# Two mixers' outputs token-major and normalised tile by tile, and an output projection that runs by tile, in a two-layer diffusion backbone

## The chip, the cores and the metric

The kernel runs on one core of one Trainium2 chip. The core has five engines that run at the same time, each with an instruction stream of its own that it works through in order: TensorE (PE in the profile; PEld is its loading of stationary operands), VectorE (DVE), ScalarE (ACT), GpSimd (POOL) and SyncE (SP, which here only issues DMAs). Matmul results go to PSUM, which has eight banks of 128 x 512 fp32. The metric is the time of one execution on the device, in microseconds (us).

## The reference

The kernel computes two trunk layers over 384 tokens: 128 of a prompt (tile 0) and 256 of a sample (tiles 1 and 2). The change lies in layer 0. There a mixer runs two groups of four heads beside each other, HGRN2 and gated DeltaNet, both in two directions; each head's output is RMS-normalised, multiplied by a gate, and all eight go through one output projection. Then follow a gated residual, a norm and an MLP.

```python
    oa_f, sa_f = hgrn_dir(f_fw, s_h[:, 0], False)
    oa_b, sa_b = hgrn_dir(f_bw, s_h[:, 1], True)
    o_a = _rmsnorm(oa_f + oa_b, gn_a) * jax.nn.silu(_heads(g_a, H_A).astype(f32))
    ...
    ob_f, sb_f = gdn_dir(a_fw, b_fw, 0, s_g[:, 0], False)
    ob_b, sb_b = gdn_dir(a_bw, b_bw, 1, s_g[:, 1], True)
    o_b = _rmsnorm(ob_f + ob_b, gn_b) * jax.nn.silu(_heads(g_b, H_B).astype(f32))
    o = jnp.concatenate([_merge(o_a), _merge(o_b)], axis=-1).astype(h.dtype)
    return (o @ w_out, ...
```

```python
        xp = xp + p_g1 * mp
        xs = xs + s_g1 * ms
        hp = _rmsnorm(xp, norm_g[l, 1]) * (1.0 + p_sc2) + p_sh2
        hs = _rmsnorm(xs, norm_g[l, 1]) * (1.0 + s_sc2) + s_sh2
        xp = xp + p_g2 * _mlp(hp, w_mlp1[l], w_mlp2[l])
        xs = xs + s_g2 * _mlp(hs, w_mlp1[l], w_mlp2[l])
```

## The kernel before

Precise products are made of three matmuls: each fp32 operand is split into a rounded part (hi) and a remainder (lo), and hi x hi, lo x hi and hi x lo are added up in PSUM. Weights are split on the fly (`split`, ACT in L211, DVE in L212) from a ring of three `raw` buffers into rings of four `whi` and four `wlo`. Plain fp32 matmuls appear in the profile as two instructions each.

A planner puts the instructions of each engine in their order: it takes what its own model holds to be ready, and among that what comes first in the program. The program's order in the mixer is the string `STEPS`: `h` advances the HGRN chain by one step, `d` the DeltaNet chain, `g0` to `g3` are the four blocks of output gates (`gate`, matmuls in `fm_block`, L647 to L649, then `evac_gate`, L1230 and L1231), `m` writes HGRN's part of the mixer's result. `ORDER` holds some matmul groups back: `("gate1", 0): [("out", 2)]` queues the first half of gate block 1 behind DeltaNet's output matmuls of tile 2. Blocks 0 and 1 are HGRN's gates, 2 and 3 DeltaNet's. All eight gate heads lie in `sg`, which is the memory of the residual stream `x` and, before that, of HGRN's keys; `x` is loaded again (`load_x`) once the gates have been used.

DeltaNet's chain is one long dependence: `gdn_attn` (L1015, L1017), `gdn_out(2)`, `gdn_out(1)`, two state steps of tile 0 (`gdn_step`, L1146 to L1177), `gdn_out(0)`. An output needs two rows of decay factors (`gdn_qg`, L1026 to L1031), then 16 or 32 small matmuls (L1188, L1191) into one bank of the tag `gd` (two banks, in turn), and one copy to SBUF (L1192). `hgrn_out` (L847 to L851) does the like with the two banks of `hg`. Both write the output with the head's features on the partitions and tokens along the row (feature-major).

So the RMS norm over features is a sum over partitions. `mix_out` makes it on TensorE, for all three tiles at once and one head at a time: squares (L1249), a matmul with a column of ones (L1251; for DeltaNet a second one with the squares of q, L1255, which carries the L2 norm's epsilon), a square root on ACT (L1258), a reciprocal on DVE (L1259), a matmul with a row of ones that spreads the factors over the partitions (L1263), a multiplication (L1265) and the split (L1266, L1267). POOL multiplies by the gates (L1256). HGRN's `mix_out` is step `m`; DeltaNet's comes after all gates.

`proj_residual` then projects with accumulators in banks 2, 3, 4 and 5 for tiles 0 and 1: for each quarter of the eight feature blocks, for both tiles, for both halves of the columns (L674 to L676). All four sums end at nearly the same time. Tile 2 follows, in pieces that `ORDER` queues behind the transposes of the next norm. `norm` calls `step(t)` for each tile, which finishes the residual (L1273, L1275), and then squares (L544), scales (L549, L550), transposes (L555), modulates (L560, L562) and splits (L564, L566, L567). The MLP's first two blocks of hidden units take tiles 0 and 1 first and tile 2 later (L1340 to L1342); their weights' splits are queued behind the norm of the first tile (`("w1", 0)`).

Of the kernel before, what the change touches and what calls it, by code (L numbers as in the profile page):

```python
# [17 lines left out]
P = 128  # L18
# [39 lines left out]
c0 h3 c1 h5 d2 h d2 h d h5 g0 g1 h d h m g2 g3 a3  # L58
# [49 lines left out]
class Trunk:  # L108
# [27 lines left out]
    def load_x(self):  # L136
        nc, i = self.nc, self.i
        nc.sync.dma_start(self.x[:, 0], i["x_prompt"][0])
        for t in range(2):
            nc.sync.dma_start(self.x[:, 1 + t], i["x_sample"][0, t * P:(t + 1) * P])  # L140
# [389 lines left out]
    def norm(self, A, B, tag, ready=None):  # L530
# [4 lines left out]
        for t in range(NT):  # L535
# [15 lines left out]
            for j in range(2):  # L551
                pt = self.ps([P, 4, P], "tmp")
                hf = self.sb([P, 4, P], self.tag_hf)
                for k in range(4):
                    self.mark["T", t, j] = nc.tensor.transpose(pt[:, k], xh[j][:, k * P:(k + 1) * P], self.c["ident"])  # L555
# [7 lines left out]
                if j:  # L563
                    self.mark["A", t] = nc.scalar.activation(hi.tiles[j][:, :, c], hf, AF.Copy)  # L564
                else:
                    nc.vector.tensor_copy(hi.tiles[j][:, :, c], hf)  # L566
                self.mark["D", t] = nc.vector.tensor_sub(lo.tiles[j][:, :, c], hf, hi.tiles[j][:, :, c].bitcast(F32))  # L567
# [273 lines left out]
    def hgrn_out(self, t, r, Sf, Sb):  # L841
# [17 lines left out]
    def mixer_tiles(self):  # L859
# [149 lines left out]
    def gdn_attn(self):  # L1009

        nc = self.nc
        for t in range(NT):
# [3 lines left out]
            for d in range(2):  # L1016
                nc.vector.tensor_mul(self.AT_[:, t, d], pk, self.AT_[:, t, d])  # L1017

# [122 lines left out]
    def gdn_step(self, t, d, S, want):  # L1141
# [28 lines left out]
        for h in range(4):  # L1170
            self.mark["s", t, d] = nc.tensor.matmul(pu[:, h], kt[:, h], ws[:, h], start=True, stop=True)
# [9 lines left out]
    def gdn_out(self, t, w, S):  # L1181
# [10 lines left out]
        nc.scalar.activation(self.vt[:, t], po, AF.Copy)  # L1192

    def gdn_steps(self):
# [15 lines left out]
        self.gdn_attn()  # L1210
        yield
# [12 lines left out]
    def evac_gate(self, n):  # L1224
# [3 lines left out]
        def f(pg):  # L1228
            s = self.cvt([P, T])
            nc.scalar.activation(s, pg, AF.Sigmoid)  # L1230
            nc.vector.scalar_tensor_tensor(self.sg[:, n], pg, self.prm[:, 12 + n // 4:13 + n // 4], s, op0=ALU.mult, op1=ALU.mult)  # L1231
        return f

    def mix_out(self, kind, y, tag):
# [3 lines left out]
        o = (self.oA, self.oB)[kind]  # L1238
        tt = lambda ap: ap.rearrange("p (t c) -> p t c", t=NT)

        one = self.mixc([P, 32], f"one{kind}")
        nc.gpsimd.memset(one, 0.0)
        nc.gpsimd.memset(one[:, 0:1], 1.0)
        e = self.mixc([P, 1], f"epsn{kind}")
        nc.gpsimd.memset(e, EPS * EPS * P if kind else EPS * P)
        st = self.ps([P, T], tag)
        for h in range(4):
            sq = self.g2([P, T])
            nc.scalar.activation(tt(sq), o[:, h], AF.Square, scale=P ** -0.5)  # L1249
            row = st[32 * h:32 * h + 32]  # L1250
# [554 lines left out]
```

## Time and profile before

| what | us |
|---|---|
| three runs | 1164.83, 1165.47, 1169.36 |
| their median | 1165.47 |
| the profiled execution, its own time | 1165.99 |
| its span, first to last instruction | 1164.2 |

The profiled execution lies 0.52 us above the median, and 1.79 us of it lie outside the span. The mean granted TensorE clock is 0.978 of full speed. The stretch of the change, from the last HGRN and DeltaNet outputs to the MLP's first matmuls, reaches from about 262 us to 404 us of the span. In the windows view each row gives a stretch, its length, and for each engine the busy time with the number of instructions in brackets (PE, PEld, DVE, ACT, POOL), then the granted clock, the busy share of the DMA engines and GB/s. In the timeline each row is a start, a length, an engine, a line of the kernel, the instruction, its output and inputs, and in brackets how long the engine had been idle and what ended that.

### The profile page before, as it was taken

The numbers are of one execution on the slowest core, as the hardware profiler recorded it, in microseconds if no ns is written. First come the engines' busy times: TensorE is split into PE (matmuls) and PEld (weight loads), VectorE is DVE, ScalarE is ACT, GpSimd is POOL, SyncE is SP. The second block draws the span as 40 slices with busy tenths as digits, with TensorE's granted clock in tenths as the row PEclk, the third lists the DMA queues.
The fourth block names the chain that finished last, engine by engine and source line by source line (L and its number), as shares of the span: only waits on it lengthen the run. The fifth ranks groups of instructions, "written<-read, shape, count | busy, mean of one in ns | idle before, by whom it ended". The sixth has DMA issues, their size and how long they took to land.

```text
span 1164.2 us, 17957 instructions
## 1 busy us (share of the span) xinstructions
PE 1102.8 (95%) x6853; PEld 940.6 (81%) x6853; DVE 766.5 (66%) x1179; ACT 493.6 (42%) x845; POOL 286.7 (25%) x309
## 2 busy tenths in 40 slices
PE   6989978998899799999999999999988999999998
PEld 3868767987866698988988878888767889999987
DVE  4587699895253788885899574877757773333333
ACT  4465323442452564334334353665635543333331
POOL 0054993231210302111112133433003011111102
PEclk9989988998998899999999999999999999999999
DMA  8954625341133287776777317665623964434301
GB/s 292 281 173 110 212 94 160 103 129 35 48 127 115 73 321 246 269 234 202 234 237 222 98 34 196 177 192 143 171 74 97 340 196 139 123 118 127 109 37 55
DMA packets 142090, 184.65 MB, mean 159 GB/s; under 512 B 36803, under 2 KB 113685, under 8 KB 142005
## 3 DMA queue, kind: packets, MB, share of 16 engines
q1 hardware_dynamic: 141685, 183.44, 50.5%
q8 instruction: 54, 0.88, 0.3%
q14 instruction: 31, 0.25, 0.1%
q10 hardware_dynamic: 320, 0.07, 0.0%
HBM read 171.53 MB, written 4.61 MB: 151 GB/s over the span
## 4 chain that ended last, share of the span: by engine, by line
PE 73%; DMA 7%; DVE 7%; POOL 7%; SPq 2%; issue 2%; ACT 1%; DVEq 0%; POOLq 0%; ACTq 0%
PE tmp L1341 7%; PE tmp L1342 7%; PE tmp L1340 7%; PE acc L1326 7%; PE acc L1327 7%; PE acc L1328 7%; POOL sm L1062 2%; POOL sm L1063 2%; DMA ada<-in_ada_w 2%; PE acc L647 2%; PE acc L648 2%; PE acc L649 2%; PE acc L675 2%; PE acc L674 2%; PE po L1715 2%
## 5 line engine op out<-in xcount | busy, mean ns | idle before, releaser
L212 DVE TENSOR_TENSOR wlo<-raw,whi 128x1024 fp32r<-128x1024 f32 x192 | 240.7, 1264 | 167.1 <-ACT whi L211 161.0
L211 ACT ACTIVATE whi<-raw 128x1024 fp32r<-128x1024 f32 x198 | 206.2, 1050 | 334.1 <-PE acc L1328 202.8
L1360 POOL TENSOR_TENSOR h<-h 128x384 f32<-128x384 f32 x56 | 66.9, 1195 | 426.4 <-ACT h L1357 423.7
L1327 PE MATMUL acc<-wlo,h 128*128 128x512 f32 x380 | 148.6, 391 | 0.0
L1326 PE MATMUL acc<-whi,h 128*128 128x512 f32 x380 | 146.1, 393 | 0.0
L349 DVE SCALAR_TENSOR_TENSOR adc<-adr,scz,adc 128x1024 f32<-128x1024 f32 x98 | 126.8, 1323 | 11.7 <-DMA adr<-in_ada_w 11.6
L1328 PE MATMUL acc<-whi,h 128*128 128x512 f32 x380 | 121.2, 391 | 0.0
L1326 PEld LDWEIGHTS acc<-whi,h 128*128 128x128 f32 x380 | 71.2, 188 | 19.7 <-ACT whi L211 5.0
L1340 PE MATMUL tmp<-hyA,whi 128*128 128x384 f32 (+1 forms) x256 | 83.8, 333 | 3.2 <-DVE hyA L566 3.2
L1341 PE MATMUL tmp<-hyA,whi 128*128 128x384 f32 (+1 forms) x256 | 84.8, 332 | 0.4 <-DVE hyA L567 0.4
L1340 PE MATMUL tmp<-hyB,whi 128*128 128x384 f32 (+1 forms) x256 | 83.7, 329 | 1.2 <-DVE hyB L566 1.2
L1341 PE MATMUL tmp<-hyB,whi 128*128 128x384 f32 (+1 forms) x256 | 84.0, 329 | 0.7 <-DVE hyB L567 0.7
L1342 PE MATMUL tmp<-hyA,wlo 128*128 128x384 f32 (+1 forms) x256 | 84.6, 332 | 0.0
L1327 PEld LDWEIGHTS acc<-wlo,h 128*128 128x128 f32 x380 | 71.4, 188 | 14.5 <-DVE wlo L212 0.8
L1342 PE MATMUL tmp<-hyB,wlo 128*128 128x384 f32 (+1 forms) x256 | 82.1, 328 | 0.0
L1328 PEld LDWEIGHTS acc<-whi,h 128*128 128x128 f32 x380 | 71.0, 188 | 13.7
L647 PE MATMUL acc<-hyA,whi 128*128 128x384 f32 x208 | 73.8, 355 | 1.4 <-DVE hyB L708 1.4
L648 PE MATMUL acc<-hyA,whi 128*128 128x384 f32 x208 | 71.9, 345 | 0.0
L649 PE MATMUL acc<-hyA,wlo 128*128 128x384 f32 x208 | 71.3, 344 | 0.0
L1361 DVE TENSOR_TENSOR h<-h,h 128x384 fp32r<-128x384 f32 (+2 forms) x72 | 38.4, 535 | 41.1 <-POOL h L1360 40.4
L1340 PEld LDWEIGHTS tmp<-hyA,whi 128*128 128x128 f32 x256 | 48.4, 191 | 4.5 <-ACT km L562 3.6
L1341 PEld LDWEIGHTS tmp<-hyA,whi 128*128 128x128 f32 x256 | 49.0, 191 | 1.6 <-DVE hyA L567 0.6
(464 smaller groups left out, 2402.5 us busy)
## 6 DMA issues: line engine op xcount, KB each, us to landing
raw<-in_w_mlp SPq DMA_DIRECT2D x128, 512.0 KB, 3.9
adr<-in_ada_w SPq DMA_DIRECT2D x80, 512.0 KB, 4.6
raw<-in_w_in_ab SPq DMA_DIRECT2D x34, 512.0 KB, 5.1
ada<-in_ada_w SPq DMA_DIRECT2D x32, 256.0 KB, 5.3
raw<-in_w_qkv_na SPq DMA_DIRECT2D x32, 256.0 KB, 3.5
raw<-in_w_out_ab SPq DMA_DIRECT2D x8, 512.0 KB, 5.3
m<-gs SPq DMA_DIRECT2D x8, 512.0 KB
raw<-in_w_qkv_na SPq DMA_DIRECT2D x8, 512.0 KB
```

Source lines behind the costliest of these rows:

```text
L211: self.nc.scalar.activation(hi, x, AF.Copy)
L212: (eng or self.nc.vector).tensor_tensor(lo, x, hi.bitcast(F32), op=ALU.subtract)
L349: nc.vector.scalar_tensor_tensor(acc[v], raw, s[v], acc[v], op0=ALU.mult, op1=ALU.add)
L647: nc.tensor.matmul(pg[n], whi(k)[:, c], hhi[:, k], start=(k == 0), stop=False)
L648: nc.tensor.matmul(pg[n], whi(k)[:, c], hlo[:, k], start=False, stop=False)
L649: nc.tensor.matmul(pg[n], wlo(k)[:, c], hhi[:, k], start=False, stop=(k == KT - 1))
L1326: nc.tensor.matmul(pg, shi, w2hi(n)[:, o], start=start, stop=False)
L1327: nc.tensor.matmul(pg, shi, w2lo(n)[:, o], start=False, stop=False)
L1328: nc.tensor.matmul(pg, slo, w2hi(n)[:, o], start=False, stop=last)
L1340: nc.tensor.matmul(pg[n], w1hi(k)[:, c], hhi[:, k, tc_], start=(k == 0), stop=False)
L1341: nc.tensor.matmul(pg[n], w1hi(k)[:, c], hlo[:, k, tc_], start=False, stop=False)
L1342: nc.tensor.matmul(pg[n], w1lo(k)[:, c], hhi[:, k, tc_], start=False, stop=(k == KT - 1))
```

## The change

The outputs of both mixers are computed token-major: the operands of the output matmuls change places, so that tokens lie on the partitions. The norm over features is then a sum along the row. `out_norm` makes it for each tile at the end of `hgrn_out` and `gdn_out`, reading the output from PSUM: four ACT squares with a sum each, a small DVE addition, a small power on POOL (`rsqrt`), and one DVE multiplication from PSUM to SBUF. The epsilon that comes from q is summed once for all tiles in `gdn_eps`, right behind `gdn_attn`. `mix_out` now runs for one tile: four transposes, a multiplication by the gates, the split. Where the gates lie in `sg` is swapped between the two groups. The projection's program order is one half of the features for tiles 2 and 1, then DeltaNet's `mix_out` for all three tiles, then the other half tile by tile; tile 0 comes last, and the first MLP takes the tiles in the same order 2, 1, 0. The accumulators get a sixth bank. Gate blocks 0 and 1 are held behind nothing any more, blocks 2 and 3 behind DeltaNet's outputs of tiles 2 and 1. The HGRN chain's last two steps move ahead of the gates. The marks that `norm` sets count tiles in the order in which they come. In layer 1 nothing changes but the order in which `proj_residual` takes its banks.

```diff
-    ("gate1", 0): [("out", 2)],
-    ("gate1", 1): [("s", 0, 0)],
-    ("gate2", 0): [("out", 0)],
-    ("proj", 0, 2, 1): [("T", 0, 0), ("T", 0, 1)],
-    ("proj", 1, 2, 0): [("T", 1, 0), ("T", 1, 1)],
+    ("gate2", 0): [("out", 2)],
+    ("gate3", 0): [("out", 1)],
+    ("proj", 0, 1): [("T", 0, 0), ("T", 0, 1)],
+    ("proj", 1, 0): [("T", 1, 0), ("T", 1, 1)],
...
-c0 h3 c1 h5 d2 h d2 h d h5 g0 g1 h d h m g2 g3 a3
+c0 h3 c1 h5 d2 h d2 h d h7 g0 g1 d m g2 g3 a3
...
-                self.mark["out", t] = nc.tensor.matmul(po[:, h], w[d][:, h], self.AT_[:, t, d, h], start=(d == 0), stop=last)
+                self.mark["out", t] = nc.tensor.matmul(po[:, h], self.AT_[:, t, d, h], w[d][:, h], start=(d == 0), stop=last)
             if S is not None:
                 for d in range(2):
-                    nc.tensor.matmul(po[:, h], S[d][:, h], qg[d][:, h], start=False, stop=(d == 1))
-        nc.scalar.activation(self.vt[:, t], po, AF.Copy)
+                    nc.tensor.matmul(po[:, h], qg[d][:, h], S[d][:, h], start=False, stop=(d == 1))
+        self.out_norm(1, t, po, self.vt[:, t])
...
+    def gdn_eps(self):
+        pq = self.ps([P, NT, 4], "gd")
+        for h in range(4):
+            q2 = self.g2([P, NT, P])
+            nc.scalar.activation(q2, self.kq[:, :, h, 1], AF.Square, scale=(EPS * P) ** 0.5)
+            for t in range(NT):
+                nc.tensor.matmul(pq[:, t, h:h + 1], q2[:, t], self.c["ones"][:, 0:1], start=True, stop=True)
+        self.qe = self.mixc([P, NT, 4], "qe")
+        nc.vector.tensor_scalar(self.qe, pq, EPS * EPS * P, None, op0=ALU.add)
...
+    def out_norm(self, kind, t, po, out):
+        ss, rs = self.sb([P, 4], "ss4"), self.sb([P, 4], "ss4")
         for h in range(4):
+            nc.scalar.activation(out[:, h], po[:, h], AF.Square, scale=P ** -0.5, accum_out=ss[:, h:h + 1])
+        if kind:
+            nc.vector.tensor_add(ss, ss, self.qe[:, t])
+        else:
+            nc.vector.tensor_scalar(ss, ss, EPS * P, None, op0=ALU.add)
+        self.rsqrt(rs, ss)
+        nc.vector.tensor_mul(out, po, rs.unsqueeze(2).broadcast_to([P, 4, P]))
+
+    def mix_out(self, kind, t, y, tag):
+        o = (self.qa, self.vt)[kind][:, t]
+        c = slice(t * P, (t + 1) * P)
+        pt = self.ps([P, 4, P], tag)
         for h in range(4):
+            nc.tensor.transpose(pt[:, h], o[:, h], self.c["ident"])
+        v = self.g2([P, 4, P])
+        nc.vector.tensor_mul(v, pt, self.gates_of(kind)[:, :, c])
+        hi, lo = (y[n].tiles[kind][:, :, c] for n in range(2))
+        nc.scalar.activation(hi, v, AF.Copy)
+        nc.vector.tensor_sub(lo, v, hi.bitcast(F32))
+
+    def gates_of(self, kind):
+        return self.sg[:, 4 - 4 * kind:8 - 4 * kind]
...
-        pg = {(c, t): self.ps([P, 512], "acc") for c in range(2) for t in range(2)}
+        pg = {(c, t): self.ps([P, 512], "acc") for t in order[:2] for c in range(2)}
+        if late:
+            for k in range(2):
+                for t in order[:2]:
+                    for c in range(2):
+                        parts[c](pg[c, t], k, t)
+                if k == 0:
+                    for t in order:
+                        late(t)
...
-        self.banks(acc=(2, 3, 4, 5, 0), tmp=(6, 1), mix=(7, 6))
-        self.mix_out(1, yy, "mix")
-        self.load_x()
-        step = self.proj_residual(i["w_out_ab"][0], yy, scr, (("wo", "wo"), ("wo", "m12")))
-        hh = self.norm(*m2, "hyA", step)
+        self.banks(acc=(2, 3, 4, 5, 0, 7), tmp=(6, 1))
+        order = 2, 1, 0
+        step = self.proj_residual(i["w_out_ab"][0], yy, scr, (("wo", "wo"), ("wo", "m12")), order,
+                                  lambda t: self.mix_out(1, t, yy, "tmp"))
+        self.load_x(order)
+        hh = self.norm(*m2, "hyA", step, order)
```

More of the change, by code (lines that the diff above doesn't have):

```diff
@@ L134, in banks, with load_x @@
         self.bank = {tag: list(b) for tag, b in tags.items()}
[L136 to L140, printed above, removed]
+    def load_x(self, order=(0, 1, 2)):
+        i = self.i
+        for t in order:
+            self.nc.sync.dma_start(self.x[:, t], i["x_sample"][0, (t - 1) * P:t * P] if t else i["x_prompt"][0])
     @contextmanager
@@ L528, in rsqrt, with norm @@
         self.nc.gpsimd.tensor_tensor(out, x, self.eps[:, 4:5].broadcast_to(list(out.shape)), op=ALU.pow)
-    def norm(self, A, B, tag, ready=None):
+    def norm(self, A, B, tag, ready=None, order=(0, 1, 2)):
         nc = self.nc
@@ L534, in norm @@
         hi, lo = self.split_tiles(tag)
-        for t in range(NT):
+        for n, t in enumerate(order):
             if ready:
@@ L1170, in gdn_step @@
         for h in range(4):
-            self.mark["s", t, d] = nc.tensor.matmul(pu[:, h], kt[:, h], ws[:, h], start=True, stop=True)
+            nc.tensor.matmul(pu[:, h], kt[:, h], ws[:, h], start=True, stop=True)
         S2 = W[:, 1]
@@ L1210, in gdn_steps @@
         self.gdn_attn()
+        self.gdn_eps()
         yield
@@ L1275, in residual, with proj_residual @@
         eng.tensor_tensor(self.x[:, t, c], self.x[:, t, c], tmp, op=ALU.add)
-    def proj_residual(self, w, hh, scr, tags):
+    def proj_residual(self, w, hh, scr, tags, order=(0, 1, 2), late=None):
         g = self.spread_gate(scr)
@@ L1282, in proj_residual @@
         parts = [self.tm_parts(w[:, cols[0]], hh), self.tm_parts(w[:, cols[1]], hh, tags)]
[L1283 to L1287 removed]
+        pg = {(c, t): self.ps([P, 512], "acc") for t in order[:2] for c in range(2)}
[5 more added lines that the diff above has]
+                if k == 0:
+                    for t in order:
+                        late(t)
+        else:
+            for q in range(4):
+                for t in order[:2]:
+                    for c in range(2):
+                        parts[c](pg[c, t], q // 2, t, (q % 2 * 2, q % 2 * 2 + 1))
         def step(t):
             for c in range(2):
[L1291 removed]
+                if t == order[2]:
                     pg[c, t] = self.ps([P, 512], "acc")
                     for k in range(2):
[L1294 removed]
+                        with self.behind("proj", c, k):
                             parts[c](pg[c, t], k, t)
@@ L1297, in proj_residual, with mlp @@
         return step
-    def mlp(self, l, hh, fine=()):
+    def mlp(self, l, hh, fine=(), order=(0, 1, 2)):
         nc, i = self.nc, self.i
         hhi, hlo = hh
-        acc = [[self.ps([P, 512], "acc") for _ in range(2)] for _ in range(NT)]
+        acc = {t: [self.ps([P, 512], "acc") for _ in range(2)] for t in order}
         NB = DFF // 256
@@ L1370, in mlp @@
             if b < BEHIND:
-                first((0, 1))
+                first(tuple(sorted(order[:2])))
                 behind.append(first)
@@ L1374, in mlp @@
                     for f in behind:
-                        f((2,))
+                        f(order[2:])
             else:
@@ L1477, in layer0 @@
                 yy = Halves(y[0::2]), Halves(y[1::2])
-                self.mix_out(0, yy, "hg")
+                for t in range(NT):
+                    self.mix_out(0, t, yy, "hg")
         self.pump(100)
@@ L1495, in layer0 @@
         self.ada_steps = self.ada_next()
-        step = self.mlp(0, hh)
+        step = self.mlp(0, hh, order=order)
         self.pump(100)
```

56 lines of the change are left out of this document (11 added, 45 removed).

## The prediction

> **What bounds the kernel now.** I read the page first, engines' busy time and then the chain that ended last.
>
> ```profile
> PE 1102.8 (95%) x6853; PEld 940.6 (81%) x6853; DVE 766.5 (66%) x1179; ACT 493.6 (42%) x845; POOL 286.7 (25%) x309
> ...
> PE 73%; DMA 7%; DVE 7%; POOL 7%; SPq 2%; issue 2%; ACT 1%; DVEq 0%; POOLq 0%; ACTq 0%
> ```
>
> TensorE is the bound, so two things shorten the run: fewer matmuls where PE is full, and fewer holes where it isn't. Second view: the windows of the stretch that changes.
>
> ```profile
> 262.00:294.00 32.00, 28.35 (x192) 24.74 (x192) 15.40 (x32) 6.33 (x10) 4.72 (x4) 0.84 0.10 32
> 294.00:310.00 16.00, 12.49 (x86) 11.56 (x86) 3.90 (x5) 5.82 (x8) 5.65 (x4) 1.00 0.10 33
> 310.00:362.00 52.00, 52.00 (x244) 37.05 (x242) 21.91 (x25) 26.36 (x39) 8.64 (x8) 1.00 0.41 132
> 362.00:380.00 18.00, 17.23 (x57) 11.50 (x56) 9.46 (x16) 3.31 (x8) 1.31 (x1) 0.81 0.18 58
> 380.00:398.00 18.00, 12.14 (x55) 9.72 (x53) 14.24 (x24) 9.87 (x20) 6.82 (x5) 0.91 0.10 32
> 398.00:404.00 6.00, 5.61 (x33) 5.41 (x34) 4.62 (x6) 2.65 (x5) 2.93 (x2) 0.72 0.60 188
> ```
>
> PE's loss in each stretch is idle time plus busy time at a lowered clock: 3.65 + 28.35 x 0.16 = 8.2; 3.5; 0; 0.8 + 17.23 x 0.19 = 4.0; 5.9 + 12.14 x 0.09 = 7.0; 0.4 + 5.61 x 0.28 = 2.0. **Together 24.7 us.** Between 310 and 362 there is no hole: there only removed work counts. Third view, PE's waits from 255 to 410 us, name, total, times, longest:
>
> ```profile
> PE tmp L1340 <- DVE hyA L566: 3.2, 1, 3.2
> PE tmp L555 <- DVE ss L546: 2.7, 1, 2.7
> PE gd L1156 <- POOL g L1146: 2.0, 1, 2.0
> ```
>
> The largest are the MLP's entry (tile 1's norm late), the first transposes of the norm (tile 0's squares late) and DeltaNet's state step.
>
> **The change part by part.** *Removed matmuls.* The sums over partitions (L1251, L1255) and the spreading of the factors (L1263) go. From the view of the lines, and three rows of the timeline around one pair:
>
> ```profile
> L1251 PE MATMUL hg<-g,one x8: 486/498/510, 317.4 to 324.5; 128*32 128x384 f32 x8
> ...
> L1251 PE MATMUL mix<-g,one x8: 486/498/510, 341.5 to 356.5; 128*32 128x384 f32 x8
> ```
> ```profile
> L1255 PE MATMUL mix<-g,one x8: 486/486/510, 342.2 to 358.7; 128*32 128x384 f32 x8
> ```
> ```profile
> 321.39 0.34 PE L648 MATMUL acc<-hyA,whi 128*128 128x384 f32 x1
> ...
> 321.66 0.83 PE L1251 MATMUL hg<-g,one 128*32 128x384 f32 x2
> ...
> 322.42 0.45 PE L649 MATMUL acc<-hyA,wlo 128*128 128x384 f32 x1
> ...
> 329.31 0.34 PE L649 MATMUL acc<-hyA,wlo 128*128 128x384 f32 x1
> ...
> 329.58 0.91 PE L1263 MATMUL hg<-g,ones 1*128 1x384 f32 x4
> ...
> 330.43 0.44 PE L647 MATMUL acc<-hyA,whi 128*128 128x384 f32 x1
> ```
>
> From one gate matmul's start to the next is 1.03 us with a pair between; without it, 0.17 (half the 0.34 that two overlapping ones show). A pair of L1251 or L1255 costs 0.86, and 12 pairs 10.3. Of L1263 two pairs run together for 1.12 - 0.17 = 0.95; alone one costs at most as much as an L1251 pair. Eight pairs at 0.7, between 0.48 and 0.86, are 5.6. Removed: 15.9.
>
> *Added matmuls.* 24 transposes and, in `gdn_eps`, 12 products with one moving column, two instructions each.
>
> ```profile
> 383.07 1.94 PE L555 MATMUL tmp<-ident,xh 128*128 128x128 f32 x8 [2.68 <-DVE ss L546]
> ```
> ```profile
> 269.22 0.95 PE L491 MATMUL tmp<-selc,ada 128*128 128x4 f32 x8
> ```
> ```profile
> 388.15 1.04 PE L555 MATMUL tmp<-ident,xh 128*128 128x128 f32 x8
> ```
>
> At full clock eight transposes take about 1.0: 3.0 in all. L491 has the same stationary load and four moving columns, 0.11 each: 24 make 2.7. The output matmuls only swap operands, both 128 wide, in the same number: nothing. **Net work: 15.9 - 3.0 - 2.7 = 10.2 us less**, all in stretches whose end is set by PE.
>
> *Longer holds of PSUM.* An output used to leave its bank by one copy; now the bank waits for four squares with their sums, a DVE addition, POOL's power and a multiplication.
>
> ```profile
> L961 ACT ACTIVATE cv<-tmp x12: 261/276/295, 69.7 to 86.8; 128x128 f32<-128x128 f32 x12
> L961 ACT ACTIVATION_READ_ACCUMULATOR cv<-tmp x12: 193/206/228, 69.8 to 86.9; 128x1 f32 x12
> ```
> ```profile
> L528 POOL TENSOR_TENSOR ss<-ss,eps x24: 548/1318/2789, 6.4 to 892.6; 128x1 f32<-128x1 f32 x12, 128x8 f32<-128x8 f32 x12
> ```
> ```profile
> L1192 ACT ACTIVATE hyB<-gd x3: 597/597/597, 294.2 to 316.6; 128x512 f32<-128x512 f32 x3
> ```
> ```profile
> 268.67 0.68 DVE L1152 TENSOR_TENSOR g<-gd,cs 128x512 f32<-128x512 f32 x1
> ```
>
> L961 is the same square: 4 x 0.48 = 1.93. Four elements on POOL lie between one (0.55) and eight (1.32): 0.88. The multiplication is L1152's form, 0.68. With 0.2 for the addition and 0.5 for three hand-overs the hold is 4.2, against 0.60: 3.6 more, six times. Behind the waiting ACT squares queue the next outputs' exponentials and the gates' sigmoids. What waits for the bank: the second decay row of tile 1 (behind output 2), the state step's transposes (behind output 1), HGRN's output 2, and the projection's first accumulators, which share `gd`'s and `hg`'s banks. Cover is the gates: blocks 1, 2 and 3 are 144 matmuls of 0.17, 25 us, and block 1 may now fill 262 to 294, where before it was held behind output 2. DeltaNet's own PE work after output 2 is small, so 262 to 310 should be nearly full; but the planner places fillers by its model, and it left 11.7 there with fillers at hand. Bounds for what stays lost: 0 to 11.7 plus three exposed holds, 22. I take 3.5, nearer to the full stretch from 310, as there are three times the fillers.
>
> *The mid-projection.* The reciprocal's chain at 359 to 368 us goes with its 4.0. Instead the second half of tile 2 waits, after the transposes, for a multiplication (0.68), a rounding (about 0.6, as L1192) and the hand-overs, while 8 more transposes cover 1.0: 0 to 2.5 with half clock behind it. I take 2.0. ACT's three table loads and DVE's two reciprocals that go lie beside PE: nothing. `load_x` now queues on SP behind the projection's weights; tile 2's part needs only HGRN's gates, the others the last gate product, two accumulators (about 5 us) before their residual: hidden.
>
> The price of a gap beyond itself shows in 383.07 (eight transposes in 1.94 after 2.68 idle) and in this window, whose clock is halved although PE had only short pieces of idle time:
>
> ```profile
> 284.00:288.00 4.00, 3.27 (x9) 2.23 (x9) 1.36 (x3) 0.69 (x2) 2.60 (x2) 0.50 0.00 0
> ```
>
> The Trainium skill, "TensorE: Matmul & The Clock Gate", section "HAM oscillation", asks only that PE has no idle gaps over about 3.4 us. By that rule the mid-projection wait would cost no clock, and the sum would be 0.5 us better; the trace, halved after 2.68 us, does not agree.
>
> *Projection by tile.* Before, all four accumulators ended together, and PE sat waiting for tile 0's squares.
>
> ```profile
> 377.44 0.40 PE L674 MATMUL acc<-whi,hyB 128*128 128x512 f32 x1
> ...
> 377.68 0.39 PE L675 MATMUL acc<-whi,m 128*128 128x512 f32 x1
> ```
> ```profile
> 394.35 0.40 PE L676 MATMUL acc<-m,hyB 128*128 128x512 f32 x1
> ```
> ```profile
> 397.93 0.71 PE L1340 MATMUL tmp<-hyA,whi 128*128 128x256 f32 x4 [3.18 <-DVE hyA L566]
> ```
>
> Now tile 2 ends 24 matmuls of 0.23, 5.5 us, ahead of tile 1; the wait of 2.7 and the slow clock after it, 3.8 in all, go. The next wait stays: from tile 1's last projection matmul to its normed rows it is the same chain, beside the MLP weights' splits on ACT and DVE, with the same 48 matmuls of the last tile as cover. I keep 3.2 and the 2.0 after it whole (bounds 0 and 8).
>
> *Order 2, 1, 0 in the MLP.* At its end tile 0's qk projection takes the bank that was tile 0's and is now tile 2's second half.
>
> ```profile
> 680.40 0.50 PE L1604 MATMUL acc<-whi,hyB 128*128 128x512 f32 x1
> ...
> 681.31 0.68 DVE L1273 TENSOR_TENSOR rt<-acc,m 128x512 f32<-128x512 f32 x1
> ```
>
> L1604 would wait until 681.99: 0 to 1.6, I take 0.8 as other waits follow.
>
> **Sum.** 10.2 of work and 24.7 of losses, less what is kept or new (3.5 + 2.0 + 3.2 + 2.0 + 0.8 = 11.5): 23.4. The profiled execution's own 1165.99 becomes 1142.6; it lies 0.5 above the median, so **1142**. The MLP would start near 375 instead of 398. Later stages pass the gain on: PE is full there even with all DMA engines busy,
>
> ```profile
> 420.00:440.00 20.00, 20.00 (x109) 18.00 (x108) 19.00 (x23) 9.19 (x18) 1.04 (x1) 1.00 1.00 351
> ```
>
> **The rivals.** *Only the work goes.* The holds and the planner's order keep the holes; 10.2 and the 3.8 at most are won: 1149 to 1159, middle 1152 to 1156. For it: 11.7 lost in 262 to 310 with fillers at hand. Against: every filler there had been held back by hand.
>
> *DVE takes the bound in the projection.* From the gates' end it owes two gates (0.6 each), six weight remainders and three products and remainders of the mixer (0.68 each) to 48 matmuls, 11 us.
>
> ```profile
> L212 DVE TENSOR_TENSOR wlo<-raw,whi 128x1024 fp32r<-128x1024 f32 x192 | 240.7, 1264 | 167.1 <-ACT whi L211 161.0
> ```
>
> That is 1.2 + 7.6 + 4.1 = 12.9, already more than 11. Were the remainders to stretch twofold, it is 20.5, 9.5 over; with only the work gone the time is 1166 - 10.2 + 6 to 10, about 1162 to 1166. Against: some remainders fit in before the gates' end.
>
> *The holds become the bound: slower.* Place: PE's queue, where a matmul that waits for a held bank stands in front of the fillers. Price: 3.6 each and, after the gap, a slow spell (1.1 in 380 to 398, 4.5 in 262 to 294; say 2.5). Six places make 36.6. Against it stands what is won with the old losses of 262 to 310 and the MLP's entry (16.9) left in place: 34.9 - 16.9 = 18.0. From 18 us of new loss, three of six places, the kernel is slower; with all six it is 1185. The Trainium skill, "Perfetto Trace Analysis", section "Matmuls", wants groups to rotate through banks so that one's evacuation overlaps the next's matmuls, which two banks with long holds do worse; here fillers in other banks speak against it.
>
> **How the numbers follow.** Forecast, 1135 to 1149: 0.55. Nearly every hole filled, 1131 to 1135: 0.06. Only the work: 0.27. DVE the bound: 0.07. Slower: 0.05. The range, 1133 to 1158, leaves out the last two and the ends of the others. A measurement can tell about 0.5% (5.8 us) from no change: faster 0.88, same 0.07, slower 0.05.
>
> **What would show it.** Right: the last matmul of the projection and the MLP's first some 23 us earlier; 262 to 310 full at clock 1.00 with gate block 1 in it; no PE wait at the first L555; a wait of 3 us still at the MLP's entry. Wrong: PE waiting on DVE multiplications of `out_norm` with `gd` banks, clock under 0.9 before the projection, or a wait for DVE remainders within it.

## The result, and the profile after

| | kernel before | changed kernel | ratio, 95% interval |
|---|---|---|---|
| first comparison, median of 4 and 4 runs | 1165.80 us | 1150.07 us | 0.9858, 0.9824 to 0.9892 |
| second comparison (below), 11 and 6 runs | 1168.46 us | 1147.56 us | 0.9826, 0.9799 to 0.9852 |
| profiled execution, its own time | 1165.99 us | 1152.35 us | |
| its span | 1164.2 us | 1150.6 us | |

The change makes the kernel 16 to 21 us faster. The forecast was 23.4 (1142): right in sign, too large, and the time lies inside the range. The engines of the changed kernel, from its page, and the windows of the stretch, in the columns of those shown before:

```profile
PE 1088.7 (95%) x6861; PEld 943.6 (82%) x6861; DVE 760.7 (66%) x1186; ACT 490.1 (43%) x874; POOL 289.9 (25%) x301
```
```profile
262.00:294.00 32.00, 30.78 (x230) 28.11 (x226) 18.11 (x37) 9.13 (x15) 2.16 (x3) 0.96 0.28 84
294.00:310.00 16.00, 13.89 (x64) 12.89 (x65) 3.74 (x7) 4.04 (x13) 4.83 (x4) 0.66 0.00 1
310.00:362.00 52.00, 50.12 (x298) 45.80 (x297) 26.56 (x40) 25.49 (x68) 10.54 (x9) 0.97 0.43 142
362.00:380.00 18.00, 15.66 (x76) 12.23 (x74) 13.85 (x29) 12.25 (x24) 10.88 (x6) 1.00 0.22 65
380.00:398.00 18.00, 16.46 (x119) 16.46 (x120) 9.02 (x18) 6.84 (x15) 2.11 (x5) 0.81 0.35 118
398.00:404.00 6.00, 6.00 (x38) 5.15 (x37) 5.70 (x7) 6.00 (x11) 0.00 (x0) 1.00 1.01 376
```

PE is still the bound. Its losses, idle time plus busy time at a lowered clock as before, are now 2.5, 6.8, 3.4, 2.3, 4.7 and 0: **19.7 us where there were 24.7**. 14.2 of the 24.7 were idle time and 10.5 the lowered clock; of the 19.7, idle time is 9.1 and the clock 10.6. So idle time fell and the clock's loss did not. The first window is nearly full. The second has a clock of 0.66 where it had 1.00, but the windows are fixed and the work has moved: output 2, which stood at 283 to 294 us before (decay rows L1028 at 282.76 and 293.83), now stands at 292 to 305. PE's waits from 240 to 400 us in the changed kernel (name, total, times, longest):

```profile
PE tmp L1359 <- DVE hyA L566: 2.1, 1, 2.1
PE gd L1197 <- ACT g L1039: 2.0, 1, 2.0
PE gd L1180 <- ACT g L1175: 1.9, 1, 1.9
...
PE tmp L1358 <- ACT whi L209: 1.5, 1, 1.5
```

The wait of 2.7 us at the norm's first transposes is gone. The MLP's entry still waits, now in two pieces (L1358 and L1359, 3.6 together).

A span mixes the change with what differs between any two executions. So I compare the same instructions in the two traces. PE's instructions stand in the same order in both kernels up to a state step of DeltaNet; from there on the order differs. Four marks follow, A the last step in common, B the MLP of layer 0 at full speed, C the first projections of layer 1, D the MLP of layer 1; first the kernel before, then the changed one:

```profile
260.69 1.06 PE L1156 MATMUL gd<-g,m 128*128 128x128 f32 x8
...
408.20 0.28 PE L1342 MATMUL tmp<-hyA,wlo 128*128 128x256 f32 x1
...
690.53 0.40 PE L1605 MATMUL acc<-whi,hyB 128*128 128x512 f32 x1
...
914.17 0.39 PE L1326 MATMUL acc<-whi,h 128*128 128x512 f32 x1
```
```profile
264.18 1.06 PE L1165 MATMUL gd<-g,m 128*128 128x128 f32 x8
...
391.50 0.28 PE L1360 MATMUL tmp<-hyA,wlo 128*128 128x256 f32 x1
...
674.78 0.39 PE L1625 MATMUL acc<-whi,hyB 128*128 128x512 f32 x1
...
900.83 0.39 PE L1344 MATMUL acc<-whi,h 128*128 128x512 f32 x1
```

At A the changed kernel is 3.5 us late although PE's program had been the same until then. From A to B it gains 20.2 (147.51 became 127.32), from B to C it gives back 1.0, from C to D 2.4 more. 3.5 - 20.2 + 1.0 + 2.4 = -13.3, and the spans differ by 13.6. So the stretch of the change won 20.2, not 13.6. The 3.5 at A belongs to the execution: a second trace of the same kernel is 1.6 us early at A, and its span is 1144.4.

### The profile page after: what moved, and what is told of

It reads as the page before. It is cut to its first block, busy times and chain, and to the rows that moved or that the text cites. A ratio compares the mean times of both kernels' runs of the same rounds, so it can differ in the third digit from the quotient of the medians.

```text
span 1150.6 us, 18007 instructions
## 1 busy us (share of the span) xinstructions
PE 1088.7 (95%) x6861; PEld 943.6 (82%) x6861; DVE 760.7 (66%) x1186; ACT 490.1 (43%) x874; POOL 289.9 (25%) x301
## 4 chain that ended last, share of the span: by engine, by line
PE 73%; DMA 7%; POOL 7%; DVE 6%; SPq 3%; issue 2%; ACT 2%; POOLq 0%; DVEq 0%; ACTq 0%
PE acc L1344 7%; PE tmp L1359 7%; PE tmp L1360 7%; PE acc L1346 7%; PE acc L1345 7%; PE tmp L1358 7%; POOL sm L1071 2%; POOL sm L1072 2%; DMA ada<-in_ada_w 2%; PE acc L646 2%; PE acc L647 2%; PE po L1735 2%; PE acc L673 2%; PE acc L674 1%; PE acc L648 1%
## 5 line engine op out<-in xcount | busy, mean ns | idle before, releaser
L210 DVE TENSOR_TENSOR wlo<-raw,whi 128x1024 fp32r<-128x1024 f32 x192 | 237.3, 1246 | 162.7 <-ACT whi L209 159.4
L1378 POOL TENSOR_TENSOR h<-h 128x384 f32<-128x384 f32 x56 | 69.9, 1248 | 423.7 <-ACT h L1375 408.2
L1359 PE MATMUL tmp<-hyA,whi 128*128 128x384 f32 (+1 forms) x256 | 85.2, 333 | 2.1 <-DVE hyA L566 2.1
L1358 PE MATMUL tmp<-hyA,whi 128*128 128x384 f32 (+1 forms) x256 | 84.3, 335 | 1.5 <-ACT whi L209 1.5
L1358 PE MATMUL tmp<-hyB,whi 128*128 128x384 f32 (+1 forms) x256 | 83.7, 329 | 1.2 <-DVE hyB L565 1.2
L1359 PE MATMUL tmp<-hyB,whi 128*128 128x384 f32 (+1 forms) x256 | 84.1, 329 | 0.7 <-DVE hyB L566 0.7
L526 POOL TENSOR_TENSOR ss<-ss,eps 128x1 f32<-128x1 f32 (+2 forms) x30 | 35.7, 1194 | 68.9 <-DVE ss L545 21.1
L1359 PEld LDWEIGHTS tmp<-hyA,whi 128*128 128x128 f32 x256 | 49.3, 193 | 3.3 <-DVE hyA L566 2.3
```

Source lines behind the costliest of these rows:

```text
L210: (eng or self.nc.vector).tensor_tensor(lo, x, hi.bitcast(F32), op=ALU.subtract)
L1358: nc.tensor.matmul(pg[n], w1hi(k)[:, c], hhi[:, k, tc_], start=(k == 0), stop=False)
L1359: nc.tensor.matmul(pg[n], w1hi(k)[:, c], hlo[:, k, tc_], start=False, stop=False)
```

## The experiments

Each kernel was run beside the kernel before on one chip: the first four shared one set of runs of it, the next four another, the last four a third. The table gives each kernel's median, its ratio to the kernel before, and from its one trace the time of each stretch against the trace of before above (negative is shorter). Where the first MLP matmuls come in another order there is no B, and A to C stands alone; in e11 and e12 D comes in another order too, and from C to the end of the span they are 2.5 and 2.8 us longer than before, the changed kernel's two traces 2.1 and 1.6. The last column is what each trace lost to a lowered clock from 262 to 404 us, by the sum over windows used above; before, it was 10.5.

| kernel | us | ratio, 95% interval | at A | A to B | B to C | A to C | C to D | clock |
|---|---|---|---|---|---|---|---|---|
| changed, first trace | 1150.1 | 0.9858, 0.9824 to 0.9892 | +3.5 | -20.2 | +1.0 | -19.2 | +2.4 | 10.6 |
| changed, second trace (e5) | 1147.6 | 0.9826, 0.9799 to 0.9852 | -1.6 | -21.3 | +1.5 | -19.8 | +1.9 | 9.1 |
| e1 block 1 held | 1159.5 | 0.9917, 0.9892 to 0.9941 | +3.4 | -9.7 | +1.0 | -8.7 | +2.4 | 11.7 |
| e2 eps first | 1147.6 | 0.9813, 0.9787 to 0.9839 | -0.8 | -24.4 | +0.9 | -23.5 | +1.8 | 2.4 |
| e3 block 1 behind attn | 1149.8 | 0.9835, 0.981 to 0.986 | +3.1 | -19.8 | +0.9 | -18.8 | +1.6 | 5.8 |
| e4 before, no norm | 1148.1 | 0.9821, 0.9796 to 0.9846 | +0.9 | -22.3 | +4.1 | -18.2 | +0.4 | 7.2 |
| e6 quarters | 1151.7 | 0.9845, 0.9821 to 0.987 | +0.4 | | | -20.3 | +6.0 | 6.3 |
| e7 copy first | 1156.6 | 0.9892, 0.9869 to 0.9916 | +3.2 | -14.0 | +1.8 | -12.2 | +1.5 | 11.3 |
| e8 order 0, 1, 2 | 1151.1 | 0.9845, 0.9821 to 0.9868 | +2.1 | -19.1 | -0.1 | -19.2 | +2.4 | 7.8 |
| e9 no eps | 1145.4 | 0.9803, 0.9773 to 0.9833 | +1.7 | -24.6 | +2.1 | -22.5 | +0.6 | 5.8 |
| e10 eps first, holds | 1149.5 | 0.9828, 0.9798 to 0.9859 | +1.4 | -20.5 | +1.0 | -19.5 | +3.0 | 6.1 |
| e11 eps first, splits free | 1150.9 | 0.9833, 0.9804 to 0.9863 | +4.2 | | | -21.8 | | 4.3 |
| e12 all three | 1149.6 | 0.9832, 0.9803 to 0.9862 | +1.2 | | | -18.6 | | 6.3 |

Two traces of one kernel differ by 1.1 us from A to B and by 0.6 from A to C, but the scatter is larger. From A to the decay row behind output 2 (L1037) the changed kernel, e5, e6 and e8 have the same PE instructions in the same order. The stretch takes 40.7 us in the first three (264.18 to 304.89 in the first) and 37.7 in e8:

```profile
262.81 1.06 PE L1165 MATMUL gd<-g,m 128*128 128x128 f32 x8
...
300.48 0.48 PE L1037 MATMUL gd<-g,ones 128*128 128x512 f32 x1
```

PE is idle for 3.3 us from 262 to 310 us in all four; e8 lost 3.3 us there to the clock, the others 6.0 to 6.3. So a difference of 3 us between single traces says nothing by itself, and the last column has to be read beside the others. An edit also lets the planner put other instructions into another order, so a kernel differs from its neighbour by more than its diff; where that decided, it is said.

### e1: gate block 1 held as before

```diff
+    ("gate1", 0): [("out", 2)],
+    ("gate1", 1): [("s", 0, 0)],
     ("gate2", 0): [("out", 2)],
```

> The changed kernel with gate block 1 held as before: its first half behind DeltaNet's output 2, its second behind the first state step of tile 0. Theory A (the freed block 1 ran early, at 265 to 280 us, ahead of DeltaNet's chain, and so moved the hole before output 2 instead of filling it): output 2's matmuls end some 8 us earlier, the stretch from attn to output 2 still runs at about half clock, and the time stays that of the changed kernel, 1147 to 1154. Theory B (freeing block 1 won the 8 us that the forecast gave it): 1156 to 1160.

1159.5, theory B; my first reading of the two traces (A) falls. The stretch from A to B loses 10.5 of its 20.2 us. Its timeline shows where one piece of that is, and it is the mechanism of the forecast's slower rival, a bank held by `out_norm`:

```profile
314.48 0.69 DVE L1259 TENSOR_TENSOR hyB<-gd,ss 128x512 f32<-128x512 f32 x1 [1.12 <-POOL ss L528]
...
315.31 1.06 PE L1175 MATMUL gd<-ident,m 128*128 128x128 f32 x4 [3.33 <-DVE ss L1257]
```

L1259 is here `out_norm`'s multiplication of output 1 out of its `gd` bank; it ends at 315.17, and PE, idle for 3.33 us, goes on with a state step's transposes (L1175) into that tag. (The row names L1257, a small addition of HGRN's that DVE began at 315.08.) With block 1 queued behind outputs, no gate matmul stands in front of the state step, and one hold is exposed. In the changed kernel no PE wait on `out_norm` is left in this stretch. That block 1 may run early is about half of what the change wins.

### e2 and e9: gdn_eps moved ahead of attn, and left out

```diff
-        self.gdn_attn()
         self.gdn_eps()
+        self.gdn_attn()
```

> The changed kernel with gdn_eps ahead of gdn_attn instead of behind it. Theory A (its 24 small matmuls and four squares, 288.95 to 292.2 us, stand in DeltaNet's chain between the last product of attn and the first decay row): the chain is 2 to 3 us shorter, 1146 to 1149. Rival (they lie in a hole that the chain has anyway): 1150 within 2 us, and the gap between attn's last matmul and the first decay row stays at 3 us or more.

> The changed kernel without gdn_eps: the epsilon that comes from q is left out (a constant in its place), and so are its 24 matmuls, four squares and one addition; the order of the rest is nearly the same. Theory A (gdn_eps costs by its place in DeltaNet's chain, about 3 us, not by its matmuls): the stretch from the state step at 264 us to the MLP's matmuls is 3 to 4 us shorter than in the changed kernel (20.2 and 21.3 us less than before there in its two traces), as short as with gdn_eps moved ahead of attn (24.4 less). Theory B (its matmuls are dear as well): 2 us or more beyond that. Rival (its cost lies in a hole): no shorter.

In the changed kernel's timeline the rows between attn and output 2 are these:

```profile
286.34 2.03 PE L1012 MATMUL gd<-m 128*128 128x128 f32 x16
...
288.95 3.22 PE L1024 MATMUL gd<-ones,g 128*128 128x1 f32 x24 [0.46 <-DVE m L1014]
289.85 0.52 ACT L1022 ACTIVATE g<-m 128x384 f32<-128x384 f32 x1 [5.12 <-PE gd L1024]
...
292.04 1.20 PE L1037 MATMUL gd<-g,ones 128*128 128x512 f32 x2
...
293.32 1.28 ACT L1039 ACT_TABLE_LOAD   x1 [2.94 <-PE gd L1037]
...
295.26 1.22 PE L1197 MATMUL gd<-sm,m 128*128 128x128 f32 x4 [2.03 <-ACT g L1039]
...
304.89 0.47 PE L1037 MATMUL gd<-g,ones 128*128 128x512 f32 x1
```

The fourth square (L1022) waits until the third one's products (L1024) free its buffer; only then come the last products, and behind them the first decay row (L1037), 3.7 us after attn's last product. The last row is the one behind output 2. With gdn_eps ahead of attn (e2), PE's rows are these:

```profile
284.94 2.03 PE L1012 MATMUL gd<-m 128*128 128x128 f32 x16
287.55 0.70 PE L1037 MATMUL gd<-g,ones 128*128 128x512 f32 x2 [0.58 <-DVE m L1014]
290.28 0.71 PE L1197 MATMUL gd<-sm,m 128*128 128x128 f32 x4 [2.03 <-ACT g L1039]
...
296.41 0.48 PE L1037 MATMUL gd<-g,ones 128*128 128x512 f32 x1
```

And the windows of this stage, first the changed kernel, then e2:

```profile
286.00:290.00 4.00, 3.54 (x33) 3.48 (x32) 2.48 (x5) 0.15 (x1) 0.00 (x0) 1.00 0.02 8
290.00:294.00 4.00, 3.23 (x18) 2.51 (x18) 2.96 (x8) 1.06 (x2) 0.00 (x0) 0.65 0.02 4
294.00:298.00 4.00, 2.50 (x8) 2.02 (x8) 0.77 (x2) 1.79 (x3) 1.28 (x1) 0.50 0.00 0
```
```profile
286.00:290.00 4.00, 1.67 (x11) 1.07 (x9) 3.68 (x6) 1.66 (x2) 0.00 (x0) 1.00 0.00 0
290.00:294.00 4.00, 2.65 (x13) 1.74 (x14) 1.83 (x2) 0.82 (x2) 2.54 (x2) 1.00 0.01 4
```

The decay row now follows 0.6 us behind attn's last product instead of 3.7, and from A to B e2 is 3.1 to 4.2 us shorter than the two traces of the changed kernel. But the shorter link is not what it wins. Set beside the first trace of the changed kernel, from A (264.18; 259.85 in e2, 262.40 in e9):

| stretch | changed | e2 | e9 |
|---|---|---|---|
| A to the start of attn's last products | 22.16 | 25.09 | 22.39 |
| from there to the first decay row | 5.70 | 2.61 | 2.61 |
| from there to the row behind output 2 | 12.85 | 8.86 | 11.30 |
| sum | 40.71 | 36.56 | 36.30 |

What the link saves, 3.1, the same products cost in front of attn, 2.9. The 4.0 of output 2's own stage are the clock: PE waits there as long as before (2.03 us for the exponential in both), at 1.00 instead of 0.65 and 0.50. Nor does the clock go with the edit alone: e11, which has e2's order up to this row, takes 38.8 us for the 36.6, and e8, with the changed kernel's order, 37.7. How much of e2's shorter stretch is the edit's, these traces don't tell, and theory A of e2 is not shown.

e9 has no products of gdn_eps at all, but its clock fell too (0.71 from 290 to 294 us, 0.50 from 294 to 298):

```profile
287.40 0.71 PE L1037 MATMUL gd<-g,ones 128*128 128x512 f32 x2 [0.58 <-DVE m L1014]
...
298.70 0.48 PE L1037 MATMUL gd<-g,ones 128*128 128x512 f32 x1
```

From A to B it is as short as e2 (-24.6 and -24.4), theory A's number, because about 2.9 us less work and 2.4 us more in output 2's stage cancel. That the matmuls of gdn_eps cost nothing does not follow; as far as these traces tell, they cost some 3 us wherever they stand. One thing does go with gdn_eps: ACT's table load for the exponential comes behind the first decay row (293.32 above), and PE waits 2.03 us; in e9 the load ran ahead at 282.78 us, and the wait is 0.69, as before the change. Over the whole run e2, e9 and the changed kernel can't be told apart by their intervals.

### e3 and e10: fillers put into the stretch before output 2

For e3; in e10 gdn_eps stands ahead of attn as well, and the second half is held behind `("qg", 2, 0)`, the first matmul of output 2's decay rows:

```diff
+    ("gate1", 0): ["attn"],
+    ("gate1", 1): ["attn"],
     ("gate2", 0): [("out", 2)],
```

> The changed kernel with both halves of gate block 1 held behind attn's last matmul, so that 48 gate matmuls (8.3 us) can stand in the stretch from attn to output 2, which ran at a granted clock of 0.66. Theory A (want of fillers there is what was left of the loss): the loss of 294 to 310 us falls from 6.8 to under 3, 1143 to 1147. Rival (the order is not the limit, output 2's own chain of decay rows, exponentials and gated rows is): the fillers all run ahead of that chain, the hole stays behind them, 1148 to 1154.

> gdn_eps ahead of attn, and gate block 1 held: its first half behind attn's last matmul, its second behind the first matmul of output 2's first decay row. Theory A (with gdn_eps out of the way the fillers now stand in output 2's own waits, 2.0 us for an exponential and some 2 more for rows): 2 to 4 us below the kernel with gdn_eps first alone, whose ratio was 0.981. Rival (as with block 1 held behind attn alone: what is filled there is missing later): within 2 us of it.

The rival, twice. With block 1 behind attn the window of e3 is hardly better (3.2 idle, 12.83 x 0.21 = 2.7), and the same wait for the exponential stands behind the fillers:

```profile
294.00:310.00 16.00, 12.83 (x64) 11.68 (x65) 5.75 (x10) 4.22 (x13) 4.82 (x4) 0.79 0.10 34
```
```profile
PE gd L1199 <- ACT g L1041: 2.1, 1, 2.1
```

In e3's PE order the 48 gate matmuls stand in front of the decay rows, not between them. In e10 24 of them stand between the first row and the second, and a wait of 2.2 us for the exponential follows all the same. PE's idle time from 262 to 310 us is 4.3 us in e3 and 4.6 in e10, against 3.3 in the changed kernel: neither hold filled output 2's chain. e10 is 4 us longer from A to B than e2, about what it lost more to the clock (6.1 against 2.4).

### e4: the kernel before without the norm

```diff
-            sq = self.g2([P, T])
-            nc.scalar.activation(tt(sq), o[:, h], AF.Square, scale=P ** -0.5)
-            row = st[32 * h:32 * h + 32]
-            nc.tensor.matmul(row, one, sq, start=True, stop=(kind == 0))
...
-            nc.tensor.matmul(pb, self.c["ones"][row], rr[row], start=True, stop=True)
...
-            nc.vector.tensor_mul(tt(v), o[:, h], tt(pb))
+            nc.vector.tensor_copy(tt(v), o[:, h])
```

> The kernel before, with the RMS norm of the mixers' outputs left out: no squares, no sums over partitions, no square root, no spreading; the rest as it was. Theory A (the 20 pairs of matmuls cost the 15.9 us that the forecast gave them, and the norm's chain in 362 to 380 us costs part of its 4.0): 1146 to 1150. Rival 1 (all 20 pairs cost 0.86 or more, with the chain): 1141 to 1145. Rival 2 (they lay in holes for a good part): 1154 or more.

The median is theory A's, but on this chip the kernel before took 1168.8, so the gain was 20.8, at the edge to rival 1. From A to B it is 22.3. Its windows, summed as above, lose 20.4 where before lost 24.7; 4.3 of the 22.3 are fewer losses, and 18.0 is the work, for which the forecast had 15.9. With all 20 pairs at 0.86 it would be 17.2, so the spreading pairs (L1263, taken as 0.7) were probably guessed too cheap; such a difference of sums is good to a microsecond or two only. Of the gain, 4.1 us are given back in the MLP of layer 0.

### e5, e6: the control, and the projection by quarters

e5 is the changed kernel unaltered. e6:

```diff
-            for k in range(2):
+            for q in range(4):
                 for t in order[:2]:
                     for c in range(2):
-                        parts[c](pg[c, t], k, t)
-                if k == 0:
+                        parts[c](pg[c, t], q // 2, t, (q % 2 * 2, q % 2 * 2 + 1))
+                if q == 1:
```

> The changed kernel itself, as the control for the runs beside it. By the first comparison (0.9858 of the kernel before) 13 to 20 us less than the kernel before on the same chip; from the state step of tile 0 at about 264 us to the MLP's matmuls it should again take some 20 us less than before, whatever the span's beginning does.

> The changed kernel with the projection's second half of the features no longer tile by tile: tiles 2 and 1 take turns by quarter, as before, so their sums end within 1.4 us of each other. Theory A (projection by tile is what took the wait of 2.7 us at the norm's first transposes away, with its slow clock 3.8): a wait of 2 to 3 us comes back at the first transposes, 2 to 5 us above the changed kernel run beside it. Rival (the wait went because other work was moved behind the projection): no such wait, within 2 us.

e5 holds: 20.9 us below the kernel before, 21.3 from A to B. In e6 the wait at the first transposes came back, as theory A said, but the MLP's entry waits less, 1.4 instead of 3.6 (3.4 in e5); its waits, in the columns as above:

```profile
PE tmp L554 <- DVE ss L545: 2.1, 1, 2.1
...
PE tmp L1358 <- DVE hyA L565: 1.4, 1, 1.4
```

From A to C it is as short as the changed kernel (-20.3 against -19.2 and -19.8). Its 4.2 us more than e5 arise between C and D, where PE's order is the same in both. So a wait moves from the MLP's entry to the transposes. But A to C doesn't settle what projection by tile is worth: from 310 to 404 us e6's clock stood at 1.00, where e5 lost 2.8 us to it and the first trace 4.6, while e6 was idle for 6.7 us against 5.6 and 5.8. Whether the loss in layer 1 comes with the edit stays open too; all four runs of e6 (1149.5 to 1152.2) lie above e5's median.

### e8: the tiles in the order 0, 1, 2

```diff
-        order = 2, 1, 0
+        order = 0, 1, 2
```

> The changed kernel with projection, norm and MLP taking the tiles in the order 0, 1, 2 as before. Theory A (order 2, 1, 0 costs about 3 us later on: 0.9 at layer 1's entry, some 2 inside layer 1): from the MLP's matmuls to the end 3 us less than in the changed kernel; against that, tile 0's output, DeltaNet's last, is needed first in the second half of the projection and stalls PE by 2 to 6 us there. Sum: 0 to 4 us above the changed kernel run beside it. Rival (the loss inside layer 1 is scatter between executions): layer 1 takes the same time as in the changed kernel, 3 to 7 us above it.

The entry to layer 1 now costs nothing (-0.1 against +1.0 and +1.5), as theory A said. The 2.4 in layer 1 remain, so they are not of the tiles' order, and half of theory A falls. Its other half, an earlier need for tile 0's output, shows as 1 to 2 us from A to B, but that hides more: up to the row behind output 2 e8 was 3.0 us faster, by the clock, and from there to B it takes 90.8 us, the changed kernel's two traces 86.6 and 85.5. Of these 4 to 5 us, PE's waits show 1.1 in the projection (L673 and L1266) and 1.4 to 1.6 at the MLP's entry; the place of the rest stays open.

### e7: a copy out of PSUM first

```diff
+        nc.scalar.activation(out, po, AF.Copy)
+        sq = self.g2([P, 4, P])
         for h in range(4):
-            nc.scalar.activation(out[:, h], po[:, h], AF.Square, ...
+            nc.scalar.activation(sq[:, h], out[:, h], AF.Square, ...
...
-        nc.vector.tensor_mul(out, po, ...
+        nc.vector.tensor_mul(out, out, ...
```

> The changed kernel with each output copied from PSUM to SBUF by ACT first, and normed from there: the bank is free after 0.6 us instead of 4 to 5. Theory A (the holds are covered by gate matmuls as the changed kernel stands): within 3 us of the changed kernel run beside it. Rival (the holds make a good part of what stays lost in 262 to 350 us): 4 to 8 us below it.

Neither: 9.0 us above e5, 6 to 7 of them from A to B. Among its waits:

```profile
PE gd L1200 <- POOL g L1040: 4.7, 2, 3.1
```

PE's order changed with the edit: the first of output 1's two decay rows now stands behind 28 gate matmuls, where the changed kernel has it in front of them, and output 1 then waits for POOL's gated rows. So freeing the bank earlier won nothing here, but the run doesn't tell what a hold costs with the order unchanged; that stays open.

### e11 and e12: the weights' splits at the MLP's entry

Both also have gdn_eps ahead of attn, and e12 e10's holds:

```diff
-    ("w1", 0): [("D", 0), ("A", 0)],
```

> gdn_eps ahead of attn, and the MLP's first weight splits held behind nothing: two of the four ACT splits then stand ahead of the norm's first squares instead of between the first and the second tile's modulations. Theory A (the waits of 3.0 and 2.2 us at the MLP's entry come from those splits and their remainders on ACT, DVE and POOL, queued ahead of the second tile's modulation): these waits fall from 5 us to under 2, and the time 3 to 6 us below the kernel with gdn_eps first alone (ratio 0.981). Rival (the weights land too late, or the norm's squares wait behind the splits instead): a wait at the norm's transposes, within 2 us of it or slower.

> Both at once: gdn_eps ahead of attn, gate block 1 held behind attn and the first decay row, the MLP's first weight splits held behind nothing. If both theories hold, the two gains add up: 5 to 10 us below the kernel with gdn_eps first alone (ratio 0.981), that is a ratio of 0.973 to 0.977. Rival (what one edit frees is waited for at the next place): no lower than the better of the two alone.

The rival. In e2 the entry waits 3.0 and 2.2. In e11 these waits are gone, and a new one stands at the norm's transposes:

```profile
PE tmp L553 <- DVE km L558: 2.8, 1, 2.8
```

e11 is no shorter from A to C than e2 (-21.8 against -23.5), nor is e12 (-18.6); against e2 they lost 1.9 and 3.9 us more to the clock. No version tried beats the changed kernel by more than the intervals.

## Why the forecast was right, and where its size was off

**The sum, from A to C.** The forecast's 23.4 stand against 19.2 and 19.8. Its parts, from the first trace of the changed kernel:

| term | forecast | measured |
|---|---|---|
| net work | 10.2 | 15.2 (20.2 less the 5.0 of fewer losses) |
| losses before, 262 to 404 | 24.7 | 24.7 |
| kept in 262 to 310 | 3.5 | 9.3, of it idle 3.3, clock 6.0 (second trace: 9.6, 3.3, 6.3) |
| kept in 310 to 362 (mid-projection) | 2.0 | 3.4, of it idle 1.9, clock 1.5 (1.9, 1.9, 0) |
| kept from 362 on (MLP entry) | 5.2 | 7.0, of it idle 3.9, clock 3.1 (6.5, 3.7, 2.8) |
| entry to layer 1 | 0.8 | 1.0 |

*The step that failed* is "I take 3.5, nearer to the full stretch from 310, as there are three times the fillers". 9.3 stayed. The fillers did their part: idle time in 262 to 310 us fell from 7.2 to 3.3, and without block 1 in front A to B is 10.5 longer (e1). The clock did not do what the forecast took as given, 1.00 in a stretch nearly full: its loss there was 4.5 and is 6.0. It fell in output 2's stage, where the decay rows, the table load and the exponential keep PE waiting for 3.3 us or more whatever fillers there are (e3, e10). Over all windows the forecast kept about 8.6 us of idle time, if its 3.5 is read as idle (3.5 + 1.5 + 3.2 + 0.4), and 9.1 and 8.9 stayed; of the clock's 10.5 it named about 2 as kept (0.5 + 1.6), and 10.6 and 9.1 stayed. How long the clock stays low differs between traces with the same PE order; what decides it is open.

*The mid-projection* did not wait. The 1.9 us of idle time in 310 to 362 are a state step's (L1180, waiting for ACT's copy in L1175; 0.7 at the same place before). That the size agrees with the 2.0 is chance.

*What made up for it* is the work. By difference it is 15.2, and 14.6 in the second trace, for 10.2. Two sizes were off that way: the removed pairs (18.0 in e4 for 15.9) and the transposes (four of them take 0.35 to 0.44 us from their first start to the next instruction's, so 24 are 2.1 to 2.6 and not 3.0). gdn_eps was sized well (2.9 in e2 for 2.7). That is some 2.5 of the 5.0; the rest is open, and sums over windows are good to a microsecond or two only. So 5.0 too little work and 9.0 too little kept loss leave the sum 4 us off: the forecast came closer than its terms deserved. The first comparison's 1150.1 also lies in the range of the rival "only the work goes" (1149 to 1159), and by the sum, 15.2 of work and 5.0 of losses, the account is nearer to that rival than the time tells.

*The holds* were sized well. Output 2 in the changed kernel, timeline:

```profile
305.23 0.28 ACT L1251 ACTIVATE hyB<-gd 128x128 f32<-128x128 f32 x1 [7.26 <-PE gd L1200]
...
306.16 0.22 ACT L1251 ACTIVATION_READ_ACCUMULATOR hyB<-gd 128x1 f32 x1
...
306.45 0.15 DVE L1253 TENSOR_TENSOR ss<-ss,qe 128x4 f32<-128x4 f32 x1
...
308.19 1.04 POOL L526 TENSOR_TENSOR ss<-ss,eps 128x4 f32<-128x4 f32 x1
309.26 0.69 DVE L1257 TENSOR_TENSOR hyB<-gd,ss 128x512 f32<-128x512 f32 x1 [2.65 <-POOL ss L526]
```

From the first square to the end of the multiplication it is 4.7 us, forecast 4.2; 1.6 of it the power waited on POOL, which was busy with a gated row of output 1 until 308.23. No term had that wait, and the squares took 1.2 us instead of 1.9, so the agreement is partly luck. That the holds stay covered was right, and e1 shows how near the slower case was: with the fillers behind the outputs, one hold shows with 3.3 us. This is also where the Trainium skill ("Perfetto Trace Analysis", section "Matmuls") with its rotation through banks bears: two banks with long holds are enough only as long as matmuls for other banks stand in front.

*Projection by tile* is not shown as a gain. The forecast took 3.8 for it; the wait did go, and e6 has it back and is no longer from A to C, but with a better clock. *The MLP's entry* stayed, as forecast, and larger. *Order 2, 1, 0* cost what was said (1.0 and 1.5; e8 -0.1). *DVE as the bound* in the projection did not come; a wait for DVE's weight remainders is not among PE's waits.

**What no step of the forecast had:** layer 1. From C to D the changed kernel is 2.4 and 1.9 us longer than before. Its PE order there is another one though the code is nearly the same, and a wait stands there that the kernel before has not; first the changed kernel, then e6:

```profile
PE sc L1700 <- DMA ks<-qk: 1.4, 1, 1.4
```
```profile
PE sc L1700 <- DMA ks<-qk: 3.5, 2, 2.5
```

"Later stages pass the gain on" was true of the MLP of layer 0 (B to C: 1.0) and not of layer 1. Between kernels with the changed kernel's order there the loss runs from 1.5 (e7) to 6.0 (e6), so part of it may be scatter; why the planner turned that order round was not tried.

**The marks set beforehand.** The MLP's first matmuls come 19.4 us earlier in the span (378.53 against 397.93), 22.9 from A, forecast 23. 262 to 294 is full with block 1 in it, 294 to 310 is not: half right. No wait at the first norm transposes: right. A wait at the MLP's entry: right, 3.6 for 3.2. Of the three signs of error (PE waiting for `out_norm`, a clock under 0.9 before the projection, DVE's remainders) the second came, 0.66, with no wait for a held bank beside it.

## What to carry to other kernels

Split the loss of a window into idle time and clock before forecasting that it goes: here fillers took idle time away and left the clock's share as it was. Before an edit is credited with 3 us, look for two traces in which PE's order is the same and see how far they differ. Longer holds of PSUM cost nothing here as long as independent matmuls stood in front of the next user of the bank, so check where a planner has put these, not only how many there are. Compare traces between instructions that both kernels have; whole spans of one kernel differed here by 6 us, of which 5 arose before anything had changed.

## What the runs showed of the hardware

In the changed kernel the granted clock was 1.00 from 290 to 291 us, 0.60 in the next microsecond and 0.50 from 292 to 298. PE was in the middle of gdn_eps's products then, behind a single wait of 0.46 us (288.95); the wait of 2.03 us came only after the fall. In e2 the same wait of 2.03 us stands in a stretch at 1.00 throughout. So the length of a wait alone did not decide it. The Trainium skill ("TensorE: Matmul & The Clock Gate", section "HAM oscillation") asks for no gaps over about 3.4 us; the trace does not agree that shorter ones are free.

DVE and POOL slow each other when both work on SBUF. The same forms alone and beside the other engine, first in e5, then in e2:

```profile
353.03 1.30 POOL L1283 TENSOR_TENSOR x<-x,g 128x512 f32<-128x512 f32 x1 [17.20 <-DVE g L1281]
...
364.87 4.55 POOL L1283 TENSOR_TENSOR x<-x,g 128x512 f32<-128x512 f32 x1 [1.66 <-DVE g L1281]
```
```profile
370.21 2.36 POOL L210 TENSOR_TENSOR wlo<-raw,whi 128x1024 fp32r<-128x1024 f32 x1 [3.27 <-ACT whi L209]
370.48 2.63 DVE L566 TENSOR_TENSOR hyA<-km,hyA 128x512 fp32r<-128x512 f32 x1
...
373.64 0.68 DVE L566 TENSOR_TENSOR hyA<-km,hyA 128x512 fp32r<-128x512 f32 x1
```

1.30 against 4.55 (DVE worked on L566 and L210 from 364.71 to 368.27), and 0.68 against 2.63; L566 is what PE waits for at the MLP's entry. The Trainium skill ("SBUF — State Buffer", section "Who interferes with whom") says that a DVE instruction with two SBUF inputs contends with a GpSimd instruction that reads SBUF, and that contention on the ports they share is an exclusive lock. The trace agrees: POOL's row ends at 372.57, and 0.68 after that is 373.25, where L566 ended at 373.11. The four squares with their sums run into each other: a pair starts every 0.26 us (305.23 to 306.16 for the first start to the last read), where the sum of the two instructions had let me expect 0.48.
